# An RWKV chunk chain with even heads on partitions 0-63 and odd heads on 64-127

## The chip, the cores and the metric

The program runs on one core of one Trainium2 chip. Every time is in device microseconds (us) of one execution on that core. TensorE does the matrix products (PE; its weight loads are listed apart as PEld), VectorE (DVE), ScalarE (ACT) and GpSimd (POOL) the rest, and nearly all transfers are issued from SyncE's queue (SPq).

## The reference, cut to what matters

The model is a hybrid decoder trunk of 1024 tokens, width 1024, float32. Its second layer mixes with RWKV-7, 8 heads of 64: per token a 64x64 state of each head is decayed, corrected by a rank-one term and read.

```python
def step(st, inp):
    r_t, w_t, k_t, v_t, kk_t, a_t = inp
    sa = jnp.einsum("bhvk,bhk->bhv", st, -kk_t)
    st = (st * w_t[:, :, None, :] + sa[..., None] * (kk_t * a_t)[:, :, None, :]
          + v_t[..., None] * k_t[:, :, None, :])
    return st, jnp.einsum("bhvk,bhk->bhv", st, r_t)
```

## The kernel before, in words

The tokens are cut into two halves of 512 (`hf` 0 and 1). Each half of the RWKV scan is a generator, `rwkv(hf, st)`, woven into the dense products of a SwiGLU FFN of the other half: `weave` advances the FFN by one step (four or eight k-tiles of weights, three float32r products of 128x128 by 128x512 for each k-tile and output tile: lines 372, 373 and 374, tiles `pg`, `pu` and `py`) and then the generator by some steps. The build's scheduler then sets the final order of each engine's instructions; an engine works through its own in that order.

The scan works on chunks of 64 tokens, 8 for a half. Before the chunks, an `am` phase forms the products within each chunk: line 1371 multiplies 64-row pieces of `kb` and `zr` for an even and an odd head in turns, into two banks `pAs[0]` and `pAs[1]` (tile `ps_A`), and stores the masked results to `w1d` and `amd` in device memory. A triangular solve on DVE follows. Then each chunk c runs through six functions, called in this order: `chain1(c)`, `prep1(c+1)`, `chain2(c)`, `prep2(c+1)`, `chain3(c)`, `prep3(c+1)`.

- `prep1` loads the chunk's matrices `w1`, `arb`, `aoff` and `xn` and transposes `kb` (and, for two chunks at once, `v`) on PE: `ps_bk`, `ps_v`.
- `prep2` and `prep3` finish the 64x64 inverse `tt` from 32x32 blocks: `ps_m` of line 1453 (`m1`, copied out by ACT), and `ps_m` of line 1463 (`m2`, copied out by DVE).
- `chain1`: `ps_g` (line 1474) is `w1` times a 128-row tile whose rows 0-63 are the state S and rows 64-127 are v. Its rows 0-63 become `g`; its rows 64-127 wait for `chain3`.
- `chain2`: `ps_u` (line 1484) is `tt` times g, and DVE copies it below v into `uv`.
- `chain3`: `ps_S` (line 1495) is `bk` times `uv`; two DVE operations (lines 1500 and 1501) make the next state. Line 1504 adds `arb` times u to `ps_g`, and ACT copies it to `ytm`.

After each second chunk, `gn` normalises 128 rows of `ytm` on DVE (lines 1547 to 1558, with a square on ACT) and multiplies by the gate on PE (`ps_gg`, `ps_yT`). In this layout all 8 heads stand side by side on the free axis, 512 elements wide on 64 partitions, and each product takes one head.

A float32 product is listed as two PE instructions, so 8 heads are 16 instructions in a row of the trace.

Of the kernel before, what the change touches and what calls it, by code (L numbers as in the profile page):

```python
# [5 lines left out]
F32 = mybir.dt.float32  # L6
# [19 lines left out]
GROUPS = (2, 2, 2, 2, 1, 1, 1)  # L26
HELD = (2, 2, 2, 2, 2, 1)
NB = 1
BUFS = dict(h=8, m=28, act=5, raw=3, w=4, tf=3, sg=2, st=3, z=6,
            xb=2, xdt=2, xd=2, y=3, dec=4, yo=1, live=4)  # L30

# [57 lines left out]
class Trunk:  # L89
# [1173 lines left out]
    def rwkv(self, hf, st):  # L1263
        nc, op = self.nc, self.op
        wdad, gd, r, k, v = st["wdad"], st["gd"], st["r"], st["k"], st["v"]
        TP = lambda n, shape, b=1: self.oq.tile(shape, F32, name=n, tag=n, bufs=b)
# [32 lines left out]
        el = TP("el", [P, 4, 8])  # L1299
# [10 lines left out]
            as_.append(a)  # L1310
        yield

        w1d = self.dr.tile([8, P, 8, P], F32, name=f"w1d{hf}")
        amd = self.dr.tile([8, 64, 8, P], F32, name=f"amd{hf}")
        psb = self.psm.tile([P, 512], F32, name="ps_bon", tag="pm")
        zr, kb = [], []
        for j in range(4):
# [28 lines left out]
            for c in range(4):  # L1346
                nc.tensor.matmul(psb[:, c * 8:(c + 1) * 8], r[j][:, c * P:(c + 1) * P], self.rkw[:, j, :],
                                 start=j == 0 and c == 0, stop=j == 3 and c == 3)
            for q in range(2):
                for b in range(2):  # L1350
                    nc.sync.dma_start(w1d[4 * q:4 * q + 4, :64, 2 * j + b, :].rearrange("c k t -> k c t"),
                                      zrj[q][64 * b:64 * b + 64])
            zr.append(zrj)
            kb.append(kbj)
            yield
        bon = TP("bon", [P, 4, 8])
        nc.vector.tensor_copy(bon.rearrange("p a b -> p (a b)"), psb[:, :32])
        eld = TP("eld", [64, 8, 8])
        for b in range(2):
            nc.vector.tensor_copy(eld[:, :, b::2], el[64 * b:64 * b + 64].rearrange("p j c -> p c j"))  # L1360
        amask = self.c_amask

        xd = self.dr.tile([8, 8, 2, 32, 32], F32, name=f"xd{hf}")
        for c in range(8):
            am = self.oq.tile([P, 4, 2, P], F32, name="am", tag="m4", bufs=2)
            pAs = [self.psum("ps_A") for _ in range(2)]
            last = None
            for j in range(4):
                for b in range(2):
                    rows = slice(64 * b, 64 * b + 64)  # L1370
                    last = self.after(last, nc.tensor.matmul(pAs[b][:, j * P:(j + 1) * P], kb[j][c // 4][rows, c % 4, :],
                                                             zr[j][c // 4][rows, c % 4, :], start=True, stop=True))
            for b in range(2):
                nc.vector.tensor_tensor(am[:, :, b, :], pAs[b].rearrange("p (j t) -> p j t", j=4),
                                        amask[:, None, :].to_broadcast([P, 4, P]), op=MULT)
            am8 = am.rearrange("p j b t -> p (j b) t")
            nc.sync.dma_start(w1d[c, 64:], am8[:64])
            nc.sync.dma_start(amd[c], am8[64:])
            yield
        A = self.oq.tile([P, 32, 32], F32, name="A", tag="m4", bufs=2)  # L1380
        for q in range(2):
# [7 lines left out]
        for s in range(31):  # L1389
            pr = self.m2("pr")  # L1390
            n, m = 31 - s, s + 1
# [9 lines left out]
        nc.sync.dma_start(self.gup, self.i["rwkv_g_up"][0])  # L1401
        ch = {}

        def newS():
            return TP("S", [P, H], 2)

        def prep1(c):

            q, cc = c // 4, c % 4
            e = ch[c] = {}  # L1410
            w1 = self.oq.tile([P, 8, P], F32, name="w1", tag="m4", bufs=2)
            nc.sync.dma_start(w1, w1d[c])
            arb = op.tile([P, 8, 64], F32, name="arb", tag="m", bufs=BUFS["m"])
            nc.sync.dma_start(arb[64:], amd[c, :, :, 64:])
            aoff = TP("aoff", [32, 8, 32], 2)
            nc.sync.dma_start(aoff, amd[c, :32, :, 32:64])
            xn = TP("xn", [64, 8, 32], 2)
            nc.sync.dma_start(xn[:32], xd[c, :, 0].rearrange("h s t -> s h t"))
            nc.sync.dma_start(xn[32:], xd[c, :, 1].rearrange("h s t -> s h t"))
            pt = self.psum("ps_bk")  # L1420
            for j in range(4):
                nc.tensor.transpose(pt[:, j * P:(j + 1) * P], kb[j][q][:, cc, :], self.c_ident)
            bk = self.m2("bk")
            nc.scalar.copy(bk, pt)
            uv = self.m2("uv")
            if c % 2 == 0:
                pv = self.psum("ps_v")
                for j in range(4):
                    nc.tensor.transpose(pv[:, j * P:(j + 1) * P], v[j][:, c * 64:(c + 2) * 64], self.c_ident)
                ch["ytm"], ch["vtm", c // 2] = self.m2("ytm"), self.m2("vtm")  # L1430
                ch["y", c // 2] = ch["ytm"]
                nc.scalar.copy(ch["vtm", c // 2], pv)
                src = pv[:64]
            else:
                src = ch["vtm", c // 2][64:]
            nc.scalar.copy(uv[:64], src)
            if c or hf == 0:
                self.S = newS()
            e["S"] = self.S
            nc.scalar.copy(self.S[64:], src)  # L1440
            e.update(w1=w1, arb=arb, aoff=aoff, xn=xn, bk=bk, uv=uv)

        def prep2(c):

            e = ch[c]
            xn, aoff = e["xn"], e["aoff"]
            tt = op.tile([P, 8, 64], F32, name="tt", tag="m", bufs=BUFS["m"])[:64]
            nc.gpsimd.memset(tt[32:, :, :32], 0.0)
            nc.vector.transpose(tt[:32, :, :32], xn[:32])
            nc.vector.transpose(tt[32:, :, 32:], xn[32:])  # L1450
            pm = self.psum("ps_m1")
            for h in range(8):
                nc.tensor.matmul(pm[32:64, h * 32:(h + 1) * 32], aoff[:, h, :], xn[:32, h, :], start=True, stop=True)
            m1 = TP("m1", [64, 8, 32], 2)
            nc.scalar.copy(m1[32:], pm[32:64, :256].rearrange("p (h t) -> p h t", h=8))
            e.update(tt=tt, m1=m1)

        def prep3(c):
            e = ch[c]
            tt, m1 = e["tt"], e["m1"]  # L1460
            pm = self.psum("ps_m2")
            for h in range(8):
                nc.tensor.matmul(pm[:32, h * 32:(h + 1) * 32], m1[32:, h, :], tt[32:, h, 32:], start=True, stop=True)
            nc.vector.tensor_copy(tt[:32, :, 32:], pm[:32, :256].rearrange("p (h t) -> p h t", h=8))

        def chain1(c):

            e = ch[c]
            pg = self.psum("ps_g")
            if hf == 0 and c == 0:  # L1470
                nc.gpsimd.memset(e["S"][:64], 0.0)
            for h in range(8):
                hs = slice(h * 64, (h + 1) * 64)
                nc.tensor.matmul(pg[:, hs], e["w1"][:, h, :], e["S"][:, hs], start=h == 0, stop=h == 7)
            g = self.m2("g")[:64]
            nc.scalar.copy(g, pg[:64])
            e.update(pg=pg, g=g)

        def chain2(c):
            e = ch[c]  # L1480
            pu = self.psum("ps_u")
            for h in range(8):
                hs = slice(h * 64, (h + 1) * 64)
                nc.tensor.matmul(pu[64:, hs], e["tt"][:, h, :], e["g"][:, hs], start=True, stop=True)
            nc.vector.tensor_copy(e["uv"][64:], pu[64:])

        def chain3(c):

            e = ch[c]
            bk, uv, arb, pg = e["bk"], e["uv"], e["arb"], e["pg"]  # L1490
            if not (hf == 1 and c == 7):
                pS = self.psum("ps_S")
                for h in range(8):
                    hs = slice(h * 64, (h + 1) * 64)
                    nc.tensor.matmul(pS[:64, hs], bk[:, hs], uv[:, hs], start=True, stop=True)
                if c == 7:
                    self.S = newS()
                Sn = self.S[:64] if c == 7 else ch[c + 1]["S"][:64]
                sv = Sn.rearrange("p (h v) -> p h v", h=8)
                nc.vector.tensor_tensor(Sn, e["S"][:64], pS[:64], op=ADD)  # L1500
                nc.vector.tensor_tensor(sv, sv, eld[:, c, :, None].to_broadcast([64, 8, 64]), op=MULT)
            for h in range(8):
                hs = slice(h * 64, (h + 1) * 64)
                nc.tensor.matmul(pg[64:, hs], arb[64:, h, :], uv[64:, hs], start=False, stop=h == 7, skip_group_check=True)
            nc.scalar.copy(ch["y", c // 2][64 * (c % 2):64 * (c % 2) + 64], pg[64:])
            del ch[c]

        prep1(0)
# [251 lines left out]
```

## Time and profile before

| what | value |
|---|---|
| time, median of 3 runs | 2421.0 us (2420.43 to 2425.15) |
| profiled execution | 2423.27 us, span 2421.5 us, granted clock 0.994 |
| PE busy | 2375.0 us, 98% |
| DVE, ACT, POOL busy | 1657.4, 971.4 and 252.5 us |
| chunk chains | from about 1050 to 1180 us and 1830 to 1930 us of the span |
| their products | 16 chunks; per chunk 8 heads of ps_g, ps_u, ps_S (15 chunks), line 1504, and both ps_m |

A row of the timeline gives an instruction's start, its length, engine, line and tiles, and xN where N instructions in a row were merged; the length then runs from the first start to the last end. Products overlap on PE: one lasts longer than the distance to the next start. For that reason the cost of a group is read here from start to start.

### The profile page before, as it was taken

The numbers are of one execution on the slowest core, as the hardware profiler recorded it, in microseconds if no ns is written. First come the engines' busy times: TensorE is split into PE (matmuls) and PEld (weight loads), VectorE is DVE, ScalarE is ACT, GpSimd is POOL, SyncE is SP. The second block draws the span as 40 slices with busy tenths as digits, with TensorE's granted clock in tenths as the row PEclk, the third lists the DMA queues.
The fourth block names the chain that finished last, engine by engine and source line by source line (L and its number), as shares of the span: only waits on it lengthen the run. The fifth ranks groups of instructions, "written<-read, shape, count | busy, mean of one in ns | idle before, by whom it ended". The sixth has DMA issues, their size and how long they took to land.

```text
span 2421.5 us, 34891 instructions
## 1 busy us (share of the span) xinstructions
PE 2375.0 (98%) x13115; PEld 1986.3 (82%) x13115; DVE 1657.4 (68%) x3244; ACT 971.4 (40%) x1708; POOL 252.5 (10%) x235
## 2 busy tenths in 40 slices
PE   7989999999999999999999999999999999999998
PEld 6878887888878887788888888877888888899997
DVE  7878767764566675775556668676656549887775
ACT  5444433322233555233333346442333334544442
POOL 2132121211112000100000111010000001000000
PEclk9999999999999999999999999999999999999999
DMA  5433533233245333644324443345433343433332
GB/s 166 120 91 103 158 110 105 90 111 99 83 133 172 95 110 94 169 129 119 97 83 144 144 135 92 105 114 158 140 100 91 116 138 96 122 106 104 105 105 79
DMA packets 318810, 280.28 MB, mean 116 GB/s; under 512 B 46003, under 2 KB 296009, under 8 KB 318641
## 3 DMA queue, kind: packets, MB, share of 16 engines
q1 hardware_dynamic: 317808, 277.64, 39.3%
q8 instruction: 103, 1.69, 0.3%
q0 software_dynamic: 832, 0.41, 0.1%
q14 instruction: 67, 0.54, 0.1%
HBM read 247.51 MB, written 30.49 MB: 115 GB/s over the span
## 4 chain that ended last, share of the span: by engine, by line
PE 90%; DVE 5%; DMA 2%; issue 1%; ACT 1%; SPq 1%; POOL 0%; DVEq 0%; ACTq 0%; POOLq 0%
PE py L372 6%; PE py L373 6%; PE py L374 6%; PE pu L372 5%; PE pu L373 5%; PE pg L373 5%; PE pg L374 5%; PE pu L374 5%; PE pg L372 5%; PE pi L372 5%; PE pi L373 5%; PE pi L374 5%; PE po L372 2%; PE po L373 2%; PE po L374 2%; PE py L701 2%
## 5 line engine op out<-in xcount | busy, mean ns | idle before, releaser
L350 ACT CAST whi<-raw 128x512 fp32r<-128x512 f32 (+1 forms) x663 | 408.6, 619 | 856.3 <-PE py L373 219.4
L351 DVE TENSOR_TENSOR wlo<-raw,whi 128x512 fp32r<-128x512 f32 (+1 forms) x663 | 479.3, 725 | 365.0 <-ACT whi L350 360.0
L373 PE MATMUL py<-actl,whi 128*128 128x512 f32 x624 | 248.1, 398 | 0.0
L372 PE MATMUL py<-acth,whi 128*128 128x512 f32 x624 | 244.8, 402 | 1.7 <-DVE h L519 0.8
L374 PE MATMUL py<-acth,wlo 128*128 128x512 f32 x624 | 246.3, 396 | 0.0
L372 PE MATMUL pu<-hnh,whi 128*128 128x512 f32 x560 | 223.6, 400 | 0.0
L373 PE MATMUL pu<-hnl,whi 128*128 128x512 f32 x560 | 223.1, 398 | 0.0
L374 PE MATMUL pu<-hnh,wlo 128*128 128x512 f32 x560 | 222.0, 397 | 0.0
L372 PE MATMUL pg<-hnh,whi 128*128 128x512 f32 x528 | 211.0, 400 | 0.0
L373 PE MATMUL pg<-hnl,whi 128*128 128x512 f32 x528 | 209.2, 396 | 0.0
L374 PE MATMUL pg<-hnh,wlo 128*128 128x512 f32 x528 | 208.4, 396 | 0.0
L372 PE MATMUL pi<-hnh,whi 128*128 128x512 f32 x512 | 204.3, 399 | 0.1
L373 PE MATMUL pi<-hnl,whi 128*128 128x512 f32 x512 | 203.2, 397 | 0.0
L374 PE MATMUL pi<-hnh,wlo 128*128 128x512 f32 x512 | 201.4, 395 | 0.0
L372 PEld LDWEIGHTS py<-acth,whi 128*128 128x128 f32 x624 | 117.9, 189 | 29.7 <-ACT whi L350 1.2
L374 PEld LDWEIGHTS py<-acth,wlo 128*128 128x128 f32 x624 | 118.0, 189 | 27.4
L373 PEld LDWEIGHTS py<-actl,whi 128*128 128x128 f32 x624 | 118.0, 189 | 25.6 <-DVE actl L238 0.2
L372 PEld LDWEIGHTS pu<-hnh,whi 128*128 128x128 f32 x560 | 105.3, 188 | 25.4 <-issue 2.2
L373 PEld LDWEIGHTS pu<-hnl,whi 128*128 128x128 f32 x560 | 105.3, 188 | 24.4
L374 PEld LDWEIGHTS pu<-hnh,wlo 128*128 128x128 f32 x560 | 105.4, 188 | 24.3 <-issue 0.7
L519 DVE TENSOR_TENSOR h<-h,py 128x512 f32<-128x512 f32 x144 | 97.1, 683 | 33.4 <-PE py L374 32.5
L373 PEld LDWEIGHTS pg<-hnl,whi 128*128 128x128 f32 x528 | 99.3, 188 | 23.2
(546 smaller groups left out, 4963.5 us busy)
## 6 DMA issues: line engine op xcount, KB each, us to landing
raw<-in_ffn_w_gate SPq DMA_DIRECT2D x88, 512.0 KB
raw<-in_ffn_w_up SPq DMA_DIRECT2D x88, 512.0 KB
raw<-in_ffn_w_down SPq DMA_DIRECT2D x72, 512.0 KB
raw<-in_od_w_in SPq DMA_DIRECT2D x44, 512.0 KB
raw<-in_ev_w_in SPq DMA_DIRECT2D x36, 512.0 KB
yraw<-yd SPq DMA_DIRECT2D x32, 256.0 KB
raw<-in_ev_w_out SPq DMA_DIRECT2D x16, 512.0 KB
raw<-in_ffn_w_down SPq DMA_DIRECT2D x32, 256.0 KB
```

The costliest lines, as they stand in the source:

```text
L350: nc.scalar.copy(hi[:, :m, :width], raw[:, k:k + m, :width])
L351: nc.vector.tensor_tensor(lo[:, :m, :width], raw[:, k:k + m, :width], hi[:, :m, :width].bitcast(F32), op=SUB)
L372: nc.tensor.matmul(o, wh[:, a:b], xh, start=st, stop=False)
L373: nc.tensor.matmul(o, wh[:, a:b], xl, start=False, stop=False)
L374: nc.tensor.matmul(o, wl[:, a:b], xh, start=False, stop=en)
L519: nc.vector.tensor_tensor(h[f], h[f], pp[t], op=ADD)
L701: mm(o, ah[:, c], bh, start=first and k == 0, stop=False, skip_group_check=True)
```

## The change

Even heads now live on partitions 0-63 and odd heads on 64-127, so the state, v, g, u and y tiles are 128 rows by 256 columns (four pairs of heads), not 64 by 512. Every product of a head has 64 contraction rows, 64 output rows on the same half and 64 columns, and `pairs` issues them in turns on the two halves, an even head, then an odd one, in an order that `after` fixes. Products that contracted 128 rows (v and S stacked) are split into two that add up in the same bank: `ps_g` into one for v and one for S, `ps_S` into one for v and one for u. The y part, which came out of rows 64-127 of `ps_g`, has its own tile `ps_y` and three products: for v, S and u. So 4 groups of 8 products in a chunk become 8 groups. The 32x32 products of `prep2` and `prep3` go in turns on the halves as well.

`arb` and `tt` share a tile `at`, g and u a tile `gu`. DVE's copies and state operations are 128x256 in place of 64x512; ACT's copies out of `ps_bk`, `ps_v` and `ps_y` are split by half and head parity (four of 64x256 for one of 128x512). The loads of `arb`, `aoff` and `xn` are split in two, 9 issues a chunk in place of 5; `am` is stored with 3 in place of 2, `zr` with one in place of two.

```diff
-            for q in range(2):
-                for b in range(2):
-                    nc.sync.dma_start(w1d[4 * q:4 * q + 4, :64, 2 * j + b, :].rearrange("c k t -> k c t"),
-                                      zrj[q][64 * b:64 * b + 64])
+                nc.sync.dma_start(w1d[4 * q:4 * q + 4, :, j, :].rearrange("c p t -> p c t"), zrj[q])
...
+        def pairs(o, w, x, start=True, stop=True):
+            last = None
+            for j in range(4):
+                for s in HALVES:
+                    last = self.after(last, nc.tensor.matmul(o[s, j * 64:(j + 1) * 64], w(j, s), x(j, s), start=start and j == 0,
+                                                             stop=stop, skip_group_check=True))
+        heads = lambda t, b: t.rearrange("p (j b v) -> p j b v", j=4, b=2)[:, :, b, :]
+        cols = lambda t, o=0: lambda j, s: t[s, o + j * 64:o + j * 64 + 64]
...
-            nc.scalar.copy(bk, pt)
+            for b in range(2):
+                for o in range(2):
+                    nc.scalar.copy(bk4[HALVES[b], o], heads(pt[HALVES[o]], b))
...
-            for h in range(8):
-                hs = slice(h * 64, (h + 1) * 64)
-                nc.tensor.matmul(pg[:, hs], e["w1"][:, h, :], e["S"][:, hs], start=h == 0, stop=h == 7)
-            g = self.m2("g")[:64]
-            nc.scalar.copy(g, pg[:64])
+            pairs(pg, lambda j, s: w1[s, 4 + j, :64], cols(e["v"]), stop=False)
+            pairs(pg, lambda j, s: w1[s, j, :64], cols(e["S"]), start=False)
+            gu = self.m2("gu")
+            nc.scalar.copy(gu[:, :256], pg[:, :256])
...
-            for h in range(8):
-                hs = slice(h * 64, (h + 1) * 64)
-                nc.tensor.matmul(pu[64:, hs], e["tt"][:, h, :], e["g"][:, hs], start=True, stop=True)
-            nc.vector.tensor_copy(e["uv"][64:], pu[64:])
+            pairs(pu, lambda j, s: tt[s, j, :], cols(gu))
+            nc.vector.tensor_copy(gu[:, 256:], pu[:, :256])
...
+                pairs(pS, cols(bk), cols(e["v"]), stop=False)
+                pairs(pS, cols(bk, 256), cols(gu, 256), start=False)
+                nc.vector.tensor_tensor(Sn, S, pS[:, :256], op=ADD)
+                nc.vector.tensor_tensor(sv, sv, el[:, :, c, None].to_broadcast([P, 4, 64]), op=MULT)
+            py = self.psum("ps_y")
+            pairs(py, lambda j, s: w1[s, 4 + j, 64:], cols(e["v"]), stop=False)
+            pairs(py, lambda j, s: w1[s, j, 64:], cols(S), start=False, stop=False)
+            pairs(py, lambda j, s: arb[s, j, :], cols(gu, 256), start=False)
```

In the changed file `pairs` issues from line 1408, the dense products stand one line lower (373 to 375), the two `ps_m` at 1464 and 1477, the copy of u at 1502 and the state at 1514 and 1515.

The order of PE, first half of the tokens, from the copy-out of chunk 0's u on. Before:

```order
L1484 MATMUL ps_u<-g,tt 64x64 x8
L1453 MATMUL ps_m_9717<-xn,aoff 32x32 x8
L374 MATMUL pg<-hnh_8189,wlo 128x512
...
L373 MATMUL pu<-hnl_8132,whi 128x512
L1495 MATMUL ps_S<-uv,bk 64x64 x8
L1504 MATMUL ps_g<-uv,arb 64x64 x8
L1463 MATMUL ps_m_9786<-tt,m_9726 32x32 x8
L374 MATMUL pu<-hnh_8131,wlo 128x512
```

Now:

```order
L1408 MATMUL ps_u<-gu,at 64x64 x8
L1464 MATMUL ps_m_9740<-xn,aoff 32x32 x8
L1408 MATMUL ps_S<-vv,bk 64x64 x8
L1408 MATMUL ps_y<-vv,w_9539 64x64 x8
L1408 MATMUL ps_y<-S,w_9539 64x64
L1408 MATMUL ps_S<-gu,bk 64x64 x8
L1408 MATMUL ps_y<-S,w_9539 64x64 x7
L1408 MATMUL ps_y<-gu,at 64x64 x8
L1477 MATMUL ps_m_9837<-at,m_9741 32x32 x8
L1408 MATMUL ps_g<-vv,w_9701 64x64 x8
L1408 MATMUL ps_g<-S,w_9701 64x64 x8
L1432 MATMUL ps_bk<-cst,kb 128x128 x4
```

The 21 dense products that stood between u's product and the state's, and the 25 between m2 and the next g, are gone from there: one chunk runs straight into the next. Chunks 0, 1 and 2 of each half stand like that, with 13 to 20 dense products only ahead of the next `ps_u`; from chunk 3 on 24 dense products stand again between u and m1 (4 to 7 at chunk 3), between y and m2 or between m2 and g, and between g and bk.

The order of DVE at the copy of chunk 2's u, first half of the tokens. Before:

```order
L217 SCALAR_TENSOR_TENSOR gs<-gs 128x8
L1556 TENSOR_TENSOR ytm<-ytm,gs 128x512
L1557 TENSOR_TENSOR ytm<-ytm,lng 128x512
L1485 COPY uv<-ps_u 64x512
L351 TENSOR_TENSOR wlo<-raw,whi 128x2x256
L1558 TENSOR_TENSOR ytm<-ytm,vtm 128x512
```

Now:

```order
L1572 TENSOR_TENSOR ytm<-ytm,gs 128x512
L1573 TENSOR_TENSOR ytm<-ytm,lng 128x512
L352 TENSOR_TENSOR wlo<-raw,whi 128x2x256
L1574 TENSOR_TENSOR ytm<-ytm,vtm 128x512
L1502 COPY gu<-ps_u 128x256
L1514 TENSOR_TENSOR S<-S,ps_S 128x256
L1515 TENSOR_TENSOR S<-S,el 128x256
```

In both the normalisation of chunks 0 and 1 stands ahead of the copy, now its last addition and one weight split (`wlo`) too. On PE 17 dense products stand in the change between chunk 3's `ps_bk` and chunk 2's `ps_u` (20 in the second half), and none between `ps_u` and the product that waits for the copy. Before, 21 dense products stood there as well.

More of the change, by code (lines that the diff above doesn't have):

```diff
@@ L28 @@
 NB = 1
+HALVES = (slice(0, 64), slice(64, 128))
 BUFS = dict(h=8, m=28, act=5, raw=3, w=4, tf=3, sg=2, st=3, z=6,
@@ L1357, in rwkv @@
         nc.vector.tensor_copy(bon.rearrange("p a b -> p (a b)"), psb[:, :32])
-        eld = TP("eld", [64, 8, 8])
-        for b in range(2):
-            nc.vector.tensor_copy(eld[:, :, b::2], el[64 * b:64 * b + 64].rearrange("p j c -> p c j"))
         amask = self.c_amask
@@ L1364, in rwkv @@
         for c in range(8):
-            am = self.oq.tile([P, 4, 2, P], F32, name="am", tag="m4", bufs=2)
+            am = self.oq.tile([P, 2, 4, P], F32, name="am", tag="m4", bufs=2)
             pAs = [self.psum("ps_A") for _ in range(2)]
@@ L1373, in rwkv @@
             for b in range(2):
-                nc.vector.tensor_tensor(am[:, :, b, :], pAs[b].rearrange("p (j t) -> p j t", j=4),
+                nc.vector.tensor_tensor(am[:, b], pAs[b].rearrange("p (j t) -> p j t", j=4),
                                         amask[:, None, :].to_broadcast([P, 4, P]), op=MULT)
-            am8 = am.rearrange("p j b t -> p (j b) t")
-            nc.sync.dma_start(w1d[c, 64:], am8[:64])
-            nc.sync.dma_start(amd[c], am8[64:])
+            for b in range(2):
+                nc.sync.dma_start(w1d[c, 64 * b:64 * b + 64, 4:, :], am[:64, b])
+            nc.sync.dma_start(amd[c], am[64:].rearrange("p b j t -> p (b j) t"))
             yield
@@ L1402, in rwkv @@
         ch = {}
-        def newS():
-            return TP("S", [P, H], 2)
+        V = {}
+        def pairs(o, w, x, start=True, stop=True):
[6 more added lines that the diff above has]
+        cols = lambda t, o=0: lambda j, s: t[s, o + j * 64:o + j * 64 + 64]
         def prep1(c):
@@ L1412, in prep1 @@
             nc.sync.dma_start(w1, w1d[c])
[L1413 to L1419, printed above, removed]
+            at = self.m2("at")
+            arb, tt = [at[:, o:o + 256].rearrange("p (j t) -> p j t", j=4) for o in (0, 256)]
+            aoff = TP("aoff", [P, 4, 32], 2)
+            xn = TP("xn", [P, 4, 32], 2)
+            for b in range(2):
+                r0, h4 = 64 * b, slice(4 * b, 4 * b + 4)
+                nc.sync.dma_start(arb[r0:r0 + 64], amd[c, :, h4, 64:])
+                nc.sync.dma_start(aoff[r0:r0 + 32], amd[c, :32, h4, 32:64])
+                for x in range(2):
+                    nc.sync.dma_start(xn[r0 + 32 * x:r0 + 32 * x + 32], xd[c, h4, x].rearrange("h s t -> s h t"))
             pt = self.psum("ps_bk")
@@ L1423, in prep1 @@
             bk = self.m2("bk")
-            nc.scalar.copy(bk, pt)
-            uv = self.m2("uv")
+            bk4 = bk.rearrange("p (o j t) -> p o j t", o=2, j=4)
+            for b in range(2):
+                for o in range(2):
+                    nc.scalar.copy(bk4[HALVES[b], o], heads(pt[HALVES[o]], b))
             if c % 2 == 0:
@@ L1429, in prep1 @@
                     nc.tensor.transpose(pv[:, j * P:(j + 1) * P], v[j][:, c * 64:(c + 2) * 64], self.c_ident)
-                ch["ytm"], ch["vtm", c // 2] = self.m2("ytm"), self.m2("vtm")
-                ch["y", c // 2] = ch["ytm"]
-                nc.scalar.copy(ch["vtm", c // 2], pv)
[L1433 to L1439, printed above, removed]
@@ L1440, in prep1 @@
-            nc.scalar.copy(self.S[64:], src)
-            e.update(w1=w1, arb=arb, aoff=aoff, xn=xn, bk=bk, uv=uv)
+                V[c // 2] = self.m2("vv")
+                v4 = V[c // 2].rearrange("p (d j t) -> p d j t", d=2, j=4)
+                for d in range(2):
+                    for b in range(2):
+                        nc.scalar.copy(v4[HALVES[b], d], heads(pv[HALVES[d]], b))
+                ch["vtm", c // 2], ch["y", c // 2] = self.m2("vtm"), self.m2("ytm")
+                nc.scalar.copy(ch["vtm", c // 2], pv)
@@ L1443, in prep2 @@
+            e.update(w1=w1, arb=arb, tt=tt, aoff=aoff, xn=xn, bk=bk, v=V[c // 2][:, c % 2 * 256:(c % 2 + 1) * 256])
         def prep2(c):
             e = ch[c]
[L1446 to L1450, printed above, removed]
-            pm = self.psum("ps_m1")
-            for h in range(8):
-                nc.tensor.matmul(pm[32:64, h * 32:(h + 1) * 32], aoff[:, h, :], xn[:32, h, :], start=True, stop=True)
@@ L1454, in prep2 @@
-            m1 = TP("m1", [64, 8, 32], 2)
-            nc.scalar.copy(m1[32:], pm[32:64, :256].rearrange("p (h t) -> p h t", h=8))
-            e.update(tt=tt, m1=m1)
+            xn, aoff, tt = e["xn"], e["aoff"], e["tt"]
+            for s in (0, 64):
+                nc.gpsimd.memset(tt[s + 32:s + 64, :, :32], 0.0)
+                nc.vector.transpose(tt[s:s + 32, :, :32], xn[s:s + 32])
+                nc.vector.transpose(tt[s + 32:s + 64, :, 32:], xn[s + 32:s + 64])
+            pm = self.psum("ps_m1")
@@ new lines, in prep2 @@
+            m1 = TP("m1", [P, 4, 32], 2)
+            last = None
+            for j in range(4):
+                for s in (0, 64):
+                    last = self.after(last, nc.tensor.matmul(pm[s + 32:s + 64, j * 32:(j + 1) * 32], aoff[s:s + 32, j, :],
+                                                             xn[s:s + 32, j, :], start=True, stop=True))
+            for s in (32, 96):
+                nc.scalar.copy(m1[s:s + 32], pm[s:s + 32, :128].rearrange("p (h t) -> p h t", h=4))
+            e.update(m1=m1)
@@ L1461, in prep3 @@
             pm = self.psum("ps_m2")
-            for h in range(8):
-                nc.tensor.matmul(pm[:32, h * 32:(h + 1) * 32], m1[32:, h, :], tt[32:, h, 32:], start=True, stop=True)
-            nc.vector.tensor_copy(tt[:32, :, 32:], pm[:32, :256].rearrange("p (h t) -> p h t", h=8))
+            last = None
+            for j in range(4):
+                for s in (0, 64):
+                    last = self.after(last, nc.tensor.matmul(pm[s:s + 32, j * 32:(j + 1) * 32], m1[s + 32:s + 64, j, :],
+                                                             tt[s + 32:s + 64, j, 32:], start=True, stop=True))
@@ L1466, in chain1 @@
+            for s in (0, 64):
+                nc.vector.tensor_copy(tt[s:s + 32, :, 32:], pm[s:s + 32, :128].rearrange("p (h t) -> p h t", h=4))
         def chain1(c):
             e = ch[c]
-            pg = self.psum("ps_g")
-            if hf == 0 and c == 0:
-                nc.gpsimd.memset(e["S"][:64], 0.0)
-            for h in range(8):
-                hs = slice(h * 64, (h + 1) * 64)
-                nc.tensor.matmul(pg[:, hs], e["w1"][:, h, :], e["S"][:, hs], start=h == 0, stop=h == 7)
@@ L1475, in chain1 @@
-            g = self.m2("g")[:64]
-            nc.scalar.copy(g, pg[:64])
-            e.update(pg=pg, g=g)
+            w1 = e["w1"]
+            if hf == 0 and c == 0:
+                self.S = TP("S", [P, 256], 2)
+                nc.gpsimd.memset(self.S, 0.0)
+            e["S"] = self.S
+            pg = self.psum("ps_g")
+            pairs(pg, lambda j, s: w1[s, 4 + j, :64], cols(e["v"]), stop=False)
+            pairs(pg, lambda j, s: w1[s, j, :64], cols(e["S"]), start=False)
+            gu = self.m2("gu")
@@ L1479, in chain2 @@
+            nc.scalar.copy(gu[:, :256], pg[:, :256])
+            e["gu"] = gu
         def chain2(c):
             e = ch[c]
+            gu, tt = e["gu"], e["tt"]
             pu = self.psum("ps_u")
-            for h in range(8):
-                hs = slice(h * 64, (h + 1) * 64)
-                nc.tensor.matmul(pu[64:, hs], e["tt"][:, h, :], e["g"][:, hs], start=True, stop=True)
-            nc.vector.tensor_copy(e["uv"][64:], pu[64:])
+            pairs(pu, lambda j, s: tt[s, j, :], cols(gu))
@@ L1487, in chain3 @@
+            nc.vector.tensor_copy(gu[:, 256:], pu[:, :256])
         def chain3(c):
             e = ch[c]
-            bk, uv, arb, pg = e["bk"], e["uv"], e["arb"], e["pg"]
+            w1, bk, gu, arb, S = e["w1"], e["bk"], e["gu"], e["arb"], e["S"]
             if not (hf == 1 and c == 7):
                 pS = self.psum("ps_S")
[L1493 to L1505, printed above, removed]
+                pairs(pS, cols(bk), cols(e["v"]), stop=False)
+                pairs(pS, cols(bk, 256), cols(gu, 256), start=False)
+                self.S = Sn = TP("S", [P, 256], 2)
+                sv = Sn.rearrange("p (h v) -> p h v", h=4)
@@ new lines, in chain3 @@
+                nc.vector.tensor_tensor(Sn, S, pS[:, :256], op=ADD)
[4 more added lines that the diff above has]
+            pairs(py, lambda j, s: arb[s, j, :], cols(gu, 256), start=False)
+            for b in range(2):
+                nc.scalar.copy(heads(ch["y", c // 2][HALVES[c % 2]], b), py[HALVES[b], :256].rearrange("p (j v) -> p j v", j=4))
```

## The prediction

> **What bounds the kernel now.** I read the engines' busy times first, then the busy time by stretches (length; busy of PE, PEld, DVE, ACT, POOL; clock; DMA share; GB/s), to see whether the chunk chains (here those of the first half) look like the rest.
>
> ```profile
> PE 2375.0 (98%) x13115; PEld 1986.3 (82%) x13115; DVE 1657.4 (68%) x3244; ACT 971.4 (40%) x1708; POOL 252.5 (10%) x235
> 1050.00:1180.00 130.00, 130.00 (x868) 107.17 (x867) 81.58 (x168) 44.10 (x78) 3.91 (x8) 1.00 0.43 120
> ```
>
> PE has no idle time in the chains, and no other engine is near full there. So PE time taken out of a chunk shortens the program one for one, as long as no new wait opens. What a chunk costs PE is in the timeline of chunk 0 (start, length, count).
>
> ```profile
> 1097.94 0.40 PE L373 MATMUL pg<-hnl,whi 128*128 128x512 f32 x1
> 1098.17 0.40 PE L374 MATMUL pg<-hnh,wlo 128*128 128x512 f32 x1
> 1098.50 0.69 PE L1463 MATMUL ps_m<-tt,m 32*32 32x32 f32 x16
> 1099.12 2.00 PE L1474 MATMUL ps_g<-S,w 128*128 128x64 f32 x16
> 1100.95 0.61 PE L1422 MATMUL ps_bk<-cst,kb 128*128 128x128 f32 x4
> 1101.32 0.48 PE L372 MATMUL pg<-hnh,whi 128*128 128x512 f32 x1
> 1101.63 0.39 PE L373 MATMUL pg<-hnl,whi 128*128 128x512 f32 x1
> ...
> 1105.81 0.40 PE L373 MATMUL pg<-hnl,whi 128*128 128x512 f32 x1
> 1106.13 1.14 PE L1484 MATMUL ps_u<-g,tt 64*64 64x64 f32 x16
> 1107.20 0.69 PE L1453 MATMUL ps_m<-xn,aoff 32*32 32x32 f32 x16
> 1107.82 0.50 PE L374 MATMUL pg<-hnh,wlo 128*128 128x512 f32 x1
> 1108.16 0.39 PE L372 MATMUL pg<-hnh,whi 128*128 128x512 f32 x1
> ...
> 1112.58 0.40 PE L373 MATMUL pu<-hnl,whi 128*128 128x512 f32 x1
> 1112.90 1.15 PE L1495 MATMUL ps_S<-uv,bk 128*64 128x64 f32 x16
> 1113.98 1.14 PE L1504 MATMUL ps_g<-uv,arb 64*64 64x64 f32 x16
> 1115.05 0.69 PE L1463 MATMUL ps_m<-tt,m 32*32 32x32 f32 x16
> 1115.66 0.50 PE L374 MATMUL pu<-hnh,wlo 128*128 128x512 f32 x1
> 1116.01 0.39 PE L372 MATMUL pu<-hnh,whi 128*128 128x512 f32 x1
> ```
>
> A dense product costs 0.23 (1097.94 to 1098.17). From dense start to dense start, less two dense products each: m2+g+bk 3.46-0.46 = 3.00, u+m1 2.35-0.46 = 1.89, S+y+m2 3.43-0.46 = 2.97. m2 is in there twice; without one of them (0.62, and 0.15 for its edge) a chunk costs PE **7.1 us**, 16 chunks 113 us.
>
> **What one product costs.** Mean length of one, by group:
>
> ```profile
> L1474 PE MATMUL ps_g<-S,w 128*128 128x64 f32 x64 | 7.7, 273 | 0.0
> L1484 PE MATMUL ps_u<-g,tt 64*64 64x64 f32 x64 | 4.6, 221 | 0.0
> L1463 PE MATMUL ps_m<-tt,m 32*32 32x32 f32 x66 | 3.0, 193 | 0.0
> L1371 PE MATMUL ps_A<-zr,kb 64*128 64x128 f32 x256 | 21.9, 287 | 0.0
> 1009.32 2.05 PE L1371 MATMUL ps_A<-zr,kb 64*128 64x128 f32 x30
> ```
>
> The step from one instruction to the next is (merged length - one length)/(count - 1): ps_g (2.00-0.27)/15 = 0.115, ps_u (1.14-0.22)/15 = 0.061, ps_m (0.69-0.19)/15 = 0.033. It goes with the columns of the weight (128, 64, 32). ps_A has 128 columns too, but 64 rows, in turns on the two halves: 32 instructions were issued (30 recorded), (2.05-0.29)/31 = 0.057, half of ps_g's step. So products on alternate halves run two at a time. Groups of 16 cost 1.84 (g), 0.98 (64 columns), 0.53 (32). What is left of each stretch is the change of shape: S+y+m2 2.97-(0.98+0.98+0.53) = 0.48 over 4 edges, **0.12** an edge.
>
> **The change on PE.** A 64x64 group in turns costs 8 x 0.061 = 0.49, if it pairs as ps_A does. A 32x32 group lies between 0.27 (pairs) and 0.53 (no better than now, if 0.033 is the fastest an instruction can be issued); I take the middle, 0.40, since no row shows instructions closer. Eight groups 3.9, two m groups 0.8, bk 0.37: 5.1. The order leaves 6 edges in chunks 0 to 2 (u, m1, S, m2, g, bk in one run), 8 afterwards: 5.8 and 6.1. Saved per chunk 1.25 and 1.0; 6 x 1.25 + 10 x 1.0 = **17.6 us**, 13.4 to 21.8 by the bounds of m.
>
> **What the other engines do, and the one place where they decide.** Prices of the narrower forms:
>
> ```profile
> L1455 ACT COPY m<-ps_m 32x256 f32<-32x256 f32 x5 | 1.8, 364 | 9.5 <-PE ps_m L1453 9.5
> L1464 DVE COPY tt<-ps_m 32x256 f32<-32x256 f32 x4 | 1.6, 412 | 1.6 <-PE ps_m L1463 1.6
> ```
>
> ACT's split copies are 11 a chunk (bk 4, vv 2 on average, m 2, y 2, gu), at most 0.36 each, about 4 us; they replace six wider ones, and ACT's 44 busy us of 130 above leave room. DVE does less: u and the two state operations at 0.41. SPq gets 4 issues more a chunk and `w1` is held until y is out instead of g; the next load into its buffer has a whole chunk (5.8 and 16 dense products, some 9 us), so I cost it at nothing. Without that cover a late `w1` or weight tile would stop PE by what it is late.
>
> The state's way back is covered: behind the last `ps_S` stand 7 y products, y's last group, m2 and g's v group, 0.43+0.49+0.12+0.40+0.12+0.49 = 2.0, and the two DVE operations need 0.22+0.41+0.41 = 1.0. The copy of u is covered in chunks 0 and 1: 1.6 of m1, S and y products against 0.6.
>
> Not so in chunk 2. Its copy of u stands on DVE behind the whole normalisation of chunks 0 and 1, and PE no longer has 21 dense products behind u. What this work takes, from before:
>
> ```profile
> 1138.46 0.66 DVE L1547 TENSOR_REDUCE gs<-ytm 128x8 f32<-128x512 f32 x1
> 1139.36 0.69 DVE L1549 TENSOR_TENSOR ytm<-ytm,gs 128x512 f32<-128x512 f32 x1
> ...
> 1142.30 0.68 DVE L1552 TENSOR_REDUCE gs<-gsq 128x8 f32<-128x512 f32 x1
> ...
> 1143.72 0.17 DVE L212 TENSOR_SCALAR gs<-gs 128x8 int32<-128x8 int32 x1
> 1143.92 0.17 DVE L213 TENSOR_SCALAR gs<-gs 128x8 int32<-128x8 int32 x1
> ...
> 1144.82 0.43 DVE L1449 STREAM_TRANSPOSE tt<-xn 32x256 f32<-32x256 f32 x1
> ...
> 1149.45 0.69 DVE L1556 TENSOR_TENSOR ytm<-ytm,gs 128x512 f32<-128x512 f32 x1
> 1150.18 0.69 DVE L1557 TENSOR_TENSOR ytm<-ytm,lng 128x512 f32<-128x512 f32 x1
> ```
>
> Counted from the end of chunk 1's y on PE: DVE gets m2 at 0.7, then two copies 0.6 (0.41 to 0.82), reduce, mean and subtraction 1.6, four half-size transposes 1.2 (0.87 to 1.7), the second reduce 0.7, 12 small steps of 0.20 = 2.4, two passes at 0.73, a weight split and the last addition 1.4, u's copy 0.4: done at 10.5. PE meanwhile does m2 0.52, g 1.10, bk 0.49, 17 dense 3.96, u 0.61, m1 0.52, two groups and one product 1.16: it waits at 8.4. That is a new wait of **2.1 us**, and 1.9 in the second half (20 dense, the products of g apart, PE there at 9.3; DVE has one `sg` and one split more, the last addition less: 11.2). Behind it on PE stand chunk 2's state, y, m2 and the next dense products; nothing else can fill it. Sum 4.0.
>
> A pause has a second price, seen once in this trace:
>
> ```profile
> 967.99 1.06 PE L1347 MATMUL ps_bon<-rkw,r 128*128 128x8 f32 x8 [1.85 <-POOL r L1345]
> ...
> 970.68 0.63 PE L372 MATMUL py<-acth,whi 128*128 128x512 f32 x1
> 971.11 0.63 PE L373 MATMUL py<-actl,whi 128*128 128x512 f32 x1
> ...
> 973.60 0.39 PE L373 MATMUL py<-actl,whi 128*128 128x512 f32 x1
> ```
>
> After 1.85 us idle dense products stand 0.43 apart, not 0.23, until the row at 973.60, about 3 us: some 1.5 lost. For two such waits 0 to 3.0; I take 1.5. For small waits of the same kind elsewhere (a `th` or a split ahead of a copy in chunk 1) I take 1.0, between 0 and 2.
>
> **Sum.** 2423.3 (profiled execution) - 17.6 + 4.0 + 1.5 + 1.0 = 2412.2. That execution was 2.3 over the median of 2421.0, so **2410 us**; by its own bounds 2399 (21.8 saved, no wait) to 2417 (13.4 saved, 9 of waits).
>
> **The rivals.**
>
> *The halves do not run at once (slower).* ps_A's turns write to two banks; `pairs` writes both halves into one bank, on different partitions and with different output columns, and no row of this trace shows that. If the bank admits one at a time, each group costs 0.98 again, and there are 8, not 4: 7.9 + 1.06 + 0.37 + 0.72 or 0.96 = 10.0 to 10.3 for 7.1, 16 x 3.0 = +49, and chunk 2's wait is gone under the longer products: **2470 us**. It decides from a step of about 0.04 us an instruction on (8 x 0.6 and 2.0 for the rest leave nothing once the waits are paid); paired the step is 0.031. Against it: the partitions written do not overlap. The Trainium skill, page "TensorEngine Tiling (Array Packing)", section "Restrictions and Gotchas", says that different row tiles cannot access the same PSUM bank simultaneously; by that rule this rival would be the outcome. The page "PSUM — Partial Sum Buffer", section "Terms", has different quadrants of one bank accessible at once, which speaks the other way; ps_A keeps the first rule and so cannot test it.
>
> *Issue binds (no change).* If an instruction cannot start sooner than 0.033 after the last, the closest steps seen, then groups cost 16 x 0.033 = 0.53 and m 0.53: 4.3+1.1+0.37+0.72 or 0.96 = 6.4 to 6.7, saved 16 x 0.5 = 8, and the waits of 6.5 take it back: **2419 us**. For it: ps_m may be bound by issue. Against: its 0.033 fits its 32 columns as 0.061 fits 64.
>
> *The waits do not show.* DVE's work before u's copy is shorter than my sum, or bk and m pair fully: 18 to 22 saved, 2421 - 19 = **2402 us**.
>
> **How the numbers follow.** Chances: the forecast 0.55, waits that do not show 0.13, issue binds 0.17, no pairing 0.12, others (a transfer late behind SPq's added issues) 0.03. About 0.2% (5 us) is what a measurement of this kernel tells from no change: under 2416 is faster, over 2426 slower. Faster: nine tenths of the forecast, all of 2402, a little of issue: 0.68. Same: 0.14. Slower: no pairing, the others, a tail of issue: 0.18. The range 2398 to 2424 holds all but the slow cases and the tails, 0.82; the forecast's own is 2399 to 2417.
>
> **What would show it.** ps_g, ps_u, ps_S and ps_y with 16 instructions in some 0.7 us (0.49 and one length), two starting together; an m group of about 0.6; PE idle about 2 us ahead of chunk 2's second `ps_S` group, released by DVE's copy of `gu`, once a half, with dense steps above 0.23 just behind it if the clock falls. Steps of 0.06 in the 64x64 groups would make the prediction wrong by its sign; a wait at another place, or none, by its size.

## The result

The changed kernel takes 2410.67 us (median, 2403.62 to 2414.08), the kernel before 2422.19 us beside it: a ratio of 0.9945, 95% interval [0.9932, 0.9959]. It is faster by 0.55%, some 11.5 us; the prediction was 2410 us. The profiled execution took 2410.26 us, 13.0 us less than the profiled one of before.

### The profile after

First the page's busy times, then the stretch 1050 to 1180 us in the table by stretches (length; busy time and instructions of PE, PEld, DVE, ACT, POOL; clock; DMA share; GB/s), and PE's new entry among its waits (total, times, longest):

```profile
PE 2360.3 (98%) x14123; PEld 1968.7 (82%) x14123; DVE 1649.1 (68%) x3288; ACT 981.4 (41%) x1788; POOL 257.0 (11%) x251
1050.00:1180.00 130.00, 127.48 (x1312) 104.66 (x1311) 89.05 (x214) 50.85 (x113) 5.90 (x17) 0.99 0.42 120
PE ps_S L1408 <- DVE gu L1502: 5.1, 4, 2.1
```

In the trace of before the chunk chains run from 1098 to 1268 us and from 1737 to 1908 us, not to 1180 and from 1830 to 1930 as the table ahead has it; PE had no idle time in all of them, so the prediction's reading holds. Now PE is busy for 14.7 us less with 1008 instructions more, and it has idle time in the chains; its releaser is DVE's copy of u. All 64x64 products of the chain now have one line (L1408, the helper `pairs`), so they are told apart by tile. PE from chunk 0's u to chunk 1's g, and then around the waits of chunks 1 and 2 (start, length, count, idle time before and its releaser):

```profile
1104.86 0.68 PE L1408 MATMUL ps_u<-gu,at 64*64 64x64 f32 x16
1105.47 0.44 PE L1464 MATMUL ps_m<-xn,aoff 32*32 32x32 f32 x16
1105.85 0.68 PE L1408 MATMUL ps_S<-vv,bk 64*64 64x64 f32 x16
1106.36 0.63 PE L1408 MATMUL ps_y<-vv,w 64*64 64x64 f32 x16
...
1108.74 0.68 PE L1408 MATMUL ps_g<-vv,w 64*64 64x64 f32 x16
1109.26 0.63 PE L1408 MATMUL ps_g<-S,w 64*64 64x64 f32 x16
1109.82 0.66 PE L1432 MATMUL ps_bk<-cst,kb 128*128 128x128 f32 x4
...
1117.57 0.68 PE L1408 MATMUL ps_S<-gu,bk 64*64 64x64 f32 x16 [0.41 <-DVE gu L1502]
...
1128.97 0.68 PE L1408 MATMUL ps_S<-gu,bk 64*64 64x64 f32 x16 [2.12 <-DVE gu L1502]
...
1130.16 1.07 PE L1408 MATMUL ps_y<-gu,at 64*64 64x64 f32 x14
1131.17 0.64 PE L1477 MATMUL ps_m<-at,m 32*32 32x32 f32 x16
1131.73 1.80 PE L1580 MATMUL ps_gg<-gd,gup 128*128 128x128 f32 x8
```

The first rows give the steps, the mean distance from one instruction's start to the next: (0.68 - 0.22)/15 = 0.031 us in a 64x64 group where before had 0.061, and (0.44 - 0.19)/15 = 0.017 in a 32x32 group where before had 0.033. The last rows show the price: 2.12 us idle, and behind it the same kinds of work run slower. The last 14 instructions of y stand (1.07 - 0.31)/13 = 0.058 us apart, half the speed (0.31 is the length of one of them there), and `ps_m` takes 0.64 for 0.44. In the second half the waits are 0.53 and 2.06 us. DVE just ahead of the long wait of the first half, and the clock behind it:

```profile
1126.57 0.69 DVE L1573 TENSOR_TENSOR ytm<-ytm,lng 128x512 f32<-128x512 f32 x1
1127.18 0.68 DVE L352 TENSOR_TENSOR wlo<-raw,whi 128x512 fp32r<-128x512 f32 x1
1127.78 0.68 DVE L1574 TENSOR_TENSOR ytm<-ytm,vtm 128x512 f32<-128x512 f32 x1
1128.49 0.42 DVE L1502 COPY gu<-ps_u 128x256 f32<-128x256 f32 x1
1128.00:1131.00 3.00, 2.03 (x46) 2.03 (x46) 1.73 (x4) 0.00 (x0) 0.00 (x0) 0.78 0.18 27
1131.00:1134.00 3.00, 3.00 (x33) 2.81 (x31) 0.57 (x2) 1.17 (x3) 0.00 (x0) 0.65 0.52 180
```

Cut to the slow time alone, in the first and in the second half, the clock is 0.50:

```profile
1129.70:1133.10 3.40, 3.40 (x52) 3.22 (x47) 1.41 (x4) 0.73 (x2) 0.00 (x0) 0.50 0.48 159
1764.60:1768.00 3.40, 3.40 (x62) 3.22 (x58) 1.53 (x5) 0.73 (x2) 0.00 (x0) 0.50 0.27 53
```

Behind both stretches it is back at 1.00. Each pause was followed by 3.4 us at half the clock, which costs up to 1.7.

**Where the time went.** The dense products (lines 372 to 374 before, 373 to 375 after) are as many in both kernels and in the same order but for a few stretches, so the same product can be found in both traces by counting. The 3498th and the 4284th of them stand ahead of and behind the first half's chains; before, then after:

```profile
1037.16 0.39 PE L374 MATMUL pg<-hnh,wlo 128*128 128x512 f32 x1
1283.52 0.47 PE L374 MATMUL pu<-hnh,wlo 128*128 128x512 f32 x1
```

```profile
1035.81 0.39 PE L375 MATMUL pg<-hnh,wlo 128*128 128x512 f32 x1
1277.09 0.39 PE L375 MATMUL pu<-hnh,wlo 128*128 128x512 f32 x1
```

246.36 us became 241.28: 5.1 us less. The 5863rd and 6849th stand around the second half's chains: 1689.89 to 1983.35, and 1684.62 to 1972.94, 5.1 us less again. So 10.2 of the profiled execution's 13.0 us come from the chains. The rest lies outside of them, where PE's order is the same but for one dense product in each half that moved by a few places; what stands ahead of the first chains takes from 1032.5 to 1037.7 us in the traces of this document, so 2.8 us out there say nothing of the change. These two lengths, the "chain lengths" below, are how the experiments are compared: 241.3 and 288.3 us for the change.

### The profile page after: what moved, and what is told of

It reads as the page before. It is cut to its first block, busy times and chain, and to the rows that moved or that the text cites. A ratio compares the mean times of both kernels' runs of the same rounds, so it can differ in the third digit from the quotient of the medians.

```text
span 2408.5 us, 37189 instructions
## 1 busy us (share of the span) xinstructions
PE 2360.3 (98%) x14123; PEld 1968.7 (82%) x14123; DVE 1649.1 (68%) x3288; ACT 981.4 (41%) x1788; POOL 257.0 (11%) x251
## 4 chain that ended last, share of the span: by engine, by line
PE 89%; DVE 6%; DMA 2%; issue 1%; ACT 1%; POOL 0%; SPq 0%; DVEq 0%; ACTq 0%
PE py L373 6%; PE py L374 6%; PE py L375 6%; PE pg L373 5%; PE pg L375 5%; PE pu L373 5%; PE pg L374 5%; PE pu L374 5%; PE pu L375 5%; PE pi L373 5%; PE pi L374 5%; PE pi L375 5%; PE po L373 2%; PE po L374 2%; PE po L375 2%; PE py L702 2%
## 5 line engine op out<-in xcount | busy, mean ns | idle before, releaser
L375 PEld LDWEIGHTS pg<-hnh,wlo 128*128 128x128 f32 x528 | 99.2, 188 | 23.4
L373 PEld LDWEIGHTS pg<-hnh,whi 128*128 128x128 f32 x528 | 99.3, 188 | 23.2
```

What stands on the lines that cost most here:

```text
L373: nc.tensor.matmul(o, wh[:, a:b], xh, start=st, stop=False)
L375: nc.tensor.matmul(o, wl[:, a:b], xh, start=False, stop=en)
```

## The experiments

Two theories stood at the start. Mine: 64-row products run two at a time because they are issued in turns on the two halves, and the change gives a part of that back through DVE's late copy of u and the clock behind the pause. The rivals: the turns do nothing (a short product is cheap by itself), or the clock falls because of the many short products.

### Turns taken away

```
-            for j in range(4):
-                for s in HALVES:
+            for s in HALVES:
+                for j in range(4):
```

> Every group of eight 64x64 products issues the four of the lower half first and then the four of the upper half, not in turns; the small 32x32 groups stay in turns. Theory (the gain comes from two halves running at once): the step goes back from 0.031 to about 0.061 us, with one pair left at the change of half, so a group costs some 0.46 us more; 8 groups x 16 chunks x 0.46 = 59 us more, less the 8 us of chunk-2 waits and slow clock, which the longer products cover: about 2461 us, slower than before the change. Rival (a 64-row product is short by itself and turns do not matter): step 0.031 as now, 2411 us.

2425.89 us, ratio 1.0024 [1.0015, 1.0033]; chain lengths 249.2 and 299.2, 18.7 us more than the change. Neither expected time came. PE in chunk 0:

```profile
1103.76 0.96 PE L1408 MATMUL ps_u<-gu,at 64*64 64x64 f32 x16
1104.65 0.44 PE L1464 MATMUL ps_m<-xn,aoff 32*32 32x32 f32 x16
...
1108.59 0.79 PE L1408 MATMUL ps_g<-vv,w 64*64 64x64 f32 x13
1109.39 0.74 PE L1408 MATMUL ps_g<-S,w 64*64 64x64 f32 x13
1110.06 0.66 PE L1432 MATMUL ps_bk<-cst,kb 128*128 128x128 f32 x4
```

A group alone (u, to the start of m1) takes 0.89 for 0.61, g's two groups 1.47 for 1.08, and the five groups in a row from the state to y 3.20 for 2.53: 0.13 to 0.28 a group, not 0.46. That is 1.34 a chunk and 21.4 in all, and the 18.7 are what is left of it when the waits on u shrink by 2.8 us (those of 2.1 to 1.1 and 1.2, the small ones to nothing). Within one half the instructions stand 0.058 apart, as expected; 16 of them in a row would be 0.93, but u takes 0.89 - 0.12 (the edge) = 0.77, some 0.16 less. In the trace the other half's first instruction of u starts at 1104.04, right behind the fifth of this half's eight, although it stands behind all eight in the program. PE thus does not need strict turns: it starts work on the other half by itself, three instructions ahead.

### The copy of u on ACT in chunk 2

```
-            nc.vector.tensor_copy(gu[:, 256:], pu[:, :256])
+            (nc.scalar.copy if c == 2 else nc.vector.tensor_copy)(gu[:, 256:], pu[:, :256])
```

> Chunk 2's copy of u runs on ACT in place of DVE in both halves; PE's order is the same. Theory (the two waits of 2.1 us and the slow clock behind them come from DVE's copy standing behind the normalisation): both waits go, the clock stays at 1.00 in chunk 2, 4.2 + 4.0 us less: about 2402.5 us. Rival A (the clock falls because of the many half-size products, not because of the pause): waits gone, clock dip stays, 2406.5 us. Rival B (the state's operations, still behind the normalisation on DVE, become the next wait): a new wait before the products of g or of the next state, 2409 to 2411 us.

2402.78 us, ratio 0.9928 [0.9916, 0.9941], as the theory had it. PE's order is the same, row for row, as in the change, and DVE's is too but for the copy. Its wait on u, and PE in chunk 2:

```profile
PE ps_S L1408 <- DVE gu L1502: 1.0, 2, 0.5
1127.06 0.57 PE L1408 MATMUL ps_S<-gu,bk 64*64 64x64 f32 x14
...
1128.49 0.44 PE L1477 MATMUL ps_m<-at,m 32*32 32x32 f32 x16
1128.86 1.16 PE L1580 MATMUL ps_gg<-gd,gup 128*128 128x128 f32 x8
```

Only chunk 1's small waits are left, the clock stays at 1.00 through the chains, and `ps_gg` is back at 1.16 from 1.80. The chain lengths are 237.4 and 284.5, 7.8 us less than the change: 4.2 of waits and, as the difference, **3.6 of slow clock**; the two stretches at 0.50 make 3.4 of it. Rival A (the clock falls with the short products) would have left these 3.6, and no new wait was seen (rival B). By the medians the kernel is 5.4 us under the change run again below (2408.16), whose profile shows the slow clock once, not twice.

### A longer and a shorter pause

```
+            for _ in range(3 if c == 0 else 0):
+                nc.vector.tensor_tensor(sq, sq, self.lng, op=MULT)
```

> Three more DVE passes of 128x512 (0.69 us each, on a scratch tile that nothing reads) in the normalisation of chunks 0 and 1, ahead of chunk 2's copy of u, in both halves. Wait before chunk 2's second state group: first half 2.1 + 2.2 - 0.7 (the last addition now stands behind the copy) = 3.6, second half 2.1 + 2.2 = 4.3. Theory (the clock's price is paid once for a pause, whatever its length above 2 us): 3.7 us more, 2414.4 us, slow stretch behind each wait some 5 us long as now. Rival (the price grows with the pause, about 1 us for 1 us): 7.4 us more, 2418 us.

2407.98 us, ratio 0.9954 [0.994, 0.9967]. The edit did not make the pause that it was meant to: the waits are 2.63 and 2.09 us, because the scheduler moved the copy ahead of one or two of the normalisation's last passes and the small steps filled in between the added ones. Neither expected time came, and the run says little: behind the pause of 2.63 us the clock was at 0.50 for 3.4 us, no longer than behind 2.1. The other direction puts the last addition on POOL:

```
-            nc.vector.tensor_tensor(y, y, v, op=ADD)
+            (nc.gpsimd if c == 0 else nc.vector).tensor_tensor(y, y, v, op=ADD)
```

> The last addition of the normalisation of chunks 0 and 1 runs on POOL, not on DVE. First half: it stood ahead of chunk 2's copy of u, so that copy ends 0.73 us sooner and the wait is 1.4 instead of 2.1 us; second half: it stands behind the copy, so the wait stays 2.1. Theory (any pause above about 1 us brings the clock down): dips behind both waits, 1.5 us each. Rival (only a pause near 2 us does): no clock below 1.00 behind the first wait. A PE wait for POOL's addition before the transposes behind may appear in either.

2406.77 us (one execution). The waits came as expected, 1.4 and 2.1 us; the clock stayed at 1.00 behind the first, as the rival had it, and fell to 0.82 and 0.61 (means of 3 us) behind the second. No wait for POOL's addition opened.

### The 32x32 groups without turns

The same exchange of the two loops as in the first experiment, in m1 and m2 alone.

> Only the two 32x32 groups of a chunk are issued four of one half, then four of the other; the 64x64 groups stay in turns. Theory (32x32 products pair fully, step 0.017, issue does not bind): step back to 0.033, 0.24 us more a group, 2 x 16 x 0.24 = 7.7 us more, of which the chunk-2 and chunk-1 waits take back about 1: 2417 us. Rival (32x32 groups were bound by issue and gain nothing from turns): 2411 us.

2412.90 us, ratio 0.9968 [0.9956, 0.998]; chain lengths 243.6 and 291.0, 5.0 us more. An m group takes 0.59 for 0.44:

```profile
1110.70 0.59 PE L1464 MATMUL ps_m<-xn,aoff 32*32 32x32 f32 x16
```

32 x 0.15 = 4.8, near the 5.0. More changed than these groups, though: the scheduler also moved dense products around chunk 2, the waits are now two, of 2.4 and 2.6 us, and in the second half the clock is at 0.50 for 6.8 us. The 0.15 rests on the rows, not on the sum. These groups do gain from turns, so issue does not bind them; that it is 0.15 and not 0.24 fits the other half starting early, as in the first experiment.

### The change again, and chunk 1's copy too

> The change itself once more, with nothing altered but one blank line, beside the next kernels on the same chip. Both theories: ratio to before 0.9945 as measured, two waits of about 2.1 us before chunk 2's second state group with the clock down behind them.

2408.16 us, ratio 0.9954 [0.9941, 0.9968]. The four waits are there again (2.1, 2.1 and the two small ones), but the clock fell behind the first alone. The table by stretches, behind the first and around the second:

```profile
1128.00:1131.00 3.00, 2.31 (x60) 2.20 (x62) 1.45 (x4) 0.26 (x1) 0.00 (x0) 0.78 0.24 36
1131.00:1134.00 3.00, 3.00 (x25) 2.85 (x21) 0.66 (x3) 1.06 (x3) 0.00 (x0) 0.65 0.47 167
...
1761.00:1764.00 3.00, 1.67 (x54) 1.60 (x55) 2.73 (x6) 0.02 (x1) 0.00 (x0) 1.00 0.17 27
1764.00:1767.00 3.00, 3.00 (x34) 2.73 (x33) 1.44 (x6) 1.30 (x3) 0.00 (x0) 1.00 0.59 179
```

Its second chain length is 286.5, 1.8 us under that of the change: the clock's part of one pause, seen in the same program. On the same chip, with the copy on ACT for chunks 1 and 2 (`c in (1, 2)` in the edit above):

> Chunk 1's copy of u runs on ACT too, beside chunk 2's. Theory (all four waits of the change come from DVE's copy of u being queued behind other work, and ACT is free enough at these places): the waits of 0.41 and 0.53 us go as well, no wait of the state group on u is left above 0.1 us, 0.9 us less than with chunk 2 alone, 8.3 us less than the change by the trace, ratio to before about 0.992. Rival (ACT's th and casts hold chunk 1's copy as long as DVE's work did): a wait of 0.3 to 0.6 us on ACT in its place, the same time as with chunk 2 alone.

2400.12 us, ratio 0.9921 [0.9909, 0.9934], 8.0 us under the change beside it. PE waits for no copy of u any more, the clock stays at 1.00 through the chains, and one wait is new, 0.7 us ahead of the second half's `ps_yT`.

### Which part of the array must differ

```
-  ...matmul(o[s, j * 64:(j + 1) * 64], w(j, s), x(j, s), ...
+  ...matmul(o[s, j * 64:(j + 1) * 64], w(j, HALVES[0]), x(j, HALVES[0]), ...
```

> The eight products of a 64x64 group all take weights and moving operand from partitions 0-63 (both turns the lower half's data, so the upper heads' results are left out); outputs still alternate between partitions 0-63 and 64-127, order and counts as in the change. Theory (two run at once because they use different rows of the array): no overlap, step 0.061, 0.49 us more a group, 8 x 16 x 0.49 = 63 us more, less 8 for the waits that are covered: about 2466 us. Rival (different output columns of the array suffice): step 0.031 and about 2411 us as now.

2406.20 us, ratio 0.9947 [0.9933, 0.996]: the rival. All operands come from partitions 0-63 (the kernel leaves out the upper heads' results), and the step is still 0.031:

```profile
1113.26 0.68 PE L1408 MATMUL ps_u<-gu,at 64*64 64x64 f32 x16
1113.87 0.44 PE L1464 MATMUL ps_m<-xn,aoff 32*32 32x32 f32 x16
...
1116.27 0.86 PE L1408 MATMUL ps_S<-gu,bk 64*64 64x64 f32 x16 [0.41 <-DVE gu L1502]
1116.91 1.07 PE L1408 MATMUL ps_y<-gu,at 64*64 64x64 f32 x16
```

So the two need not lie on different rows; results on different partitions are enough. (The last two rows show the clock falling behind a pause of 0.41 us. It is at 0.50 for 6.8 us here; PE so comes up to 3.4 us later to chunk 2, whose wait of 2.1 is gone.) In this kernel the two products of a turn also share weights and moving operand; the last experiment below has two on the same rows that share neither. Two row halves that write the same partitions of one bank were not tried.

### Four at a time

If different rows or different result partitions suffice, the four quarters of 64x64 might run at once. On top of the version with ACT's copies, products with one moving operand are issued together: g and y of v, g and y of S, state and y of u. y lands on the opposite half, and its copies take it from there.

```
+            for j in range(4):
+                for o, w, other in ((g, wg, 0), (y, wy, 1)):
+                    for b in range(2):
+                        s = HALVES[b]
+                        ...matmul(o[HALVES[b ^ other], js], w(j, s), x(j, s), ...
```

> Built on the version with the copies of u of chunks 1 and 2 on ACT. Products that share a moving operand are issued four in turns on the four 64x64 quarters: g and y of v, then g and y of S, then (after u) the state and y of u; y's results land on the opposite half and its copies take them from there. 5 instead of 8 runs of turns a chunk, with the same number of instructions. Theory (pairs run together because they sit on different rows or on different columns, so four quarters run four at a time): step 0.016 us in these runs, 3 x 0.49 = 1.5 us less a chunk, 23 us less than 2400: 2377 us, if no wait opens. Rival (two at a time is the most): the step stays 0.031 in them, 2400 us, give or take waits from the moved y products.

2383.93 us, ratio 0.9847 [0.9834, 0.9861]: 1.5% under the kernel before, with nothing left out. PE in chunk 0's g and y of v and of S:

```profile
1099.50 0.27 PE L1420 MATMUL ps_g<-vv,w 64*64 64x64 f32 x2
1099.51 0.27 PE L1420 MATMUL ps_y<-vv,w 64*64 64x64 f32 x2
...
1100.42 0.23 PE L1420 MATMUL ps_g<-S,w 64*64 64x64 f32 x2
1100.44 0.23 PE L1420 MATMUL ps_y<-S,w 64*64 64x64 f32 x2
1100.59 0.66 PE L1445 MATMUL ps_bk<-cst,kb 128*128 128x128 f32 x4
```

64 instructions start within 0.94 us, 0.015 apart: four at a time. Against the version it is built on the chain lengths fall by 7.3 and 8.2 us, 15.5 and not 23. In 12 of the 16 chunks the scheduler sends the first four instructions of g ahead of the others, among dense products, where they run two at a time and add changes of shape. Each chain length now has 82 changes of shape on PE, the version below it 63: 38 more at the prediction's 0.12 are some 4.6 of the missing 8 us, an estimate; the rest stays open. The same once more for u and the state's products from v:

> As the version with four quarters, and the products of the state from v are issued in turns with those of u too (u lands on the opposite half; two copies of half the partitions bring it back, on ACT in chunks 1 and 2, on DVE otherwise). Theory (four at a time): 0.49 us less a chunk, 7 us less than 2384 over 15 chunks: 2377 us. Rival (u's copy, now two of about 0.4 us with fewer products of the chain behind u on PE to cover it, opens a wait before the next state products): a wait of 0.3 to 0.8 us in some chunks, 2380 to 2386 us.

2382.87 us, ratio 0.9848 [0.983, 0.9866], which cannot be told from the one before: 7 us were expected, and the chain lengths fell by 1.3. No wait opened. Here u and the state's products from v start 0.01 us apart (1102.47 and 1102.48 in chunk 0) and run four at a time, with different weights and different moving operands on the same rows. But the first four of the state's products stand apart in the same way, and the changes of shape rise to 92 in each half, some 2.4 us more by the same estimate.

## Why the prediction was right

By its own steps, in the profiled execution:

- **PE's saving, 17.6 forecast.** The chains are 10.2 us shorter; with 5.1 us of waits and 3.6 of slow clock put back, PE's work is **18.9 us** less. The 64x64 groups came out as forecast (0.49). The 32x32 groups were mis-sized: I took the middle, 0.40, and they cost 0.27, the end at which they pair fully; that alone is 2 x 16 x 0.13 = 4.2 us more, 21.8 in all. From dense start to dense start, as the prediction measured, a chunk costs 5.6 in chunk 0 without `ps_v` (5.8 forecast) and 5.96 in chunk 3 (6.1 forecast): the later chunks have more to pay between their groups than the 8 edges. By these two chunks the saving would be 6 x 1.5 + 10 x 1.14 = 20.4; the 1.5 us between that and 18.9 I cannot place.
- **Chunk 2's waits, 4.0 forecast.** 2.12 and 2.06, at the place that was named, released by the copy that was named.
- **The clock, 1.5 forecast (0 to 3).** 3.6 in this execution, over the bound: each pause cost about 1.8 (3.4 us at half the clock). The prediction halved the one example it had; for this execution it should have taken it whole for each pause. The second profile of the same program paid once only.
- **Small waits, 1.0 forecast.** 0.41 and 0.53, in chunk 1.
- **Sum.** 2412.2 forecast, 2410.26 measured in the profiled execution; 10.2 of its 13.0 us under before are the chains, where the prediction had 17.6 - 4.0 - 1.5 - 1.0 = 11.1. The mechanism and the place of the waits were right. That the median came within 1 us of 2410 is in part luck: 1.3 us too little saving stands against 2.1 us too little slow clock, and 2.8 us outside of the chains against the 2.3 that the prediction took off for the profiled execution, which this time lay 0.4 under its median.

The rivals. *The halves do not run at once* is out: the step is 0.031 with both halves in one bank. This rival would have been the outcome by the rule in "Restrictions and Gotchas" of the Trainium skill's page "TensorEngine Tiling (Array Packing)", so for halves that write different partitions the measurement decides against that rule. *Issue binds* is out: 0.017, and later 0.015, stand under its 0.033. *The waits do not show* was wrong for this kernel, and its 2402 us is what taking them away gave.

What was right for a reason that was too narrow is the pairing itself. The prediction held the turns on two halves of the rows to be what makes it; the runs show that without turns PE finds over half of the overlap of the 64x64 groups by itself (1.34 us lost a chunk, of the 3.7 that 8 groups of 0.46 would make), and that different result partitions do as well as different rows.

Why so much better packing gave only 18.9 us can be read from the rows of before: a 128-row product (g, S) cost what two 64-row products in a pair now cost, 8 x 0.23 = 1.84 for g and y against four groups of 0.49, and 0.98 for the state against two. Only u, y's last group and the two small groups, which had 64 or 32 rows before, really got cheaper: 0.49 + 0.49 + 2 x 0.26, less the 0.12 that g and y lost, is 1.4 us a chunk, 22 in 16 chunks; the same edges and the unplaced rest lie between that and 18.9.

## What to carry to other kernels

Count what PE can run at the same time before you split a product: splitting 128 rows into two halves gained nothing here, and small products gain only as far as they fill rows and result partitions that stand idle, here up to four 64x64 quarters. When PE gets faster, look at what the engine that releases it has queued ahead of the release; one copy behind a normalisation took back 4.2 us, and the slow clock behind these pauses 3.6 more, until a free engine took the copy over.

## What was not expected of the hardware

- The two products of a pair start 4 to 7 ns apart, whether they differ in rows and result partitions or in result partitions alone, and four quarters make a step of 0.015 us.
- PE starts products on the other half three instructions before the last of this half's, so issue order matters less than expected: 0.13 to 0.28 us a group.
- A pause of PE brings the clock down in one execution and not in another. Behind the chains' pauses of 2 us and more it fell 8 times out of 9 (not behind the second in the repeated change); behind 1.1 and 1.4 us it stayed up, behind 1.2 us it fell to 0.50; behind pauses of 0.4 and 0.5 us it fell both times in the run on the lower rows, and never in the five other runs that have them. What decides it stays open. Each time the clock was at 0.50 for 3.4 or 6.8 us, whatever the pause. "What's actually happening" in the Trainium skill's page "TensorE: Matmul & The Clock Gate" has a free-running window of about 3.4 us in which activity is judged; the slow stretches here last one or two such windows, and a free-running window would fit a chance outcome for one and the same pause, which no run here shows. But the page speaks of a whole idle window, and none of these pauses was that long.
